# Set sizes 22, 14 and 8 in the last feed-forward, and weight differences formed later, in a two-layer encoder

## The chip, the cores and the metric

The kernel runs on one core of one Trainium2 chip. The metric is the device time of one execution in microseconds (us). Engines are named as in the profile: PE is TensorE (PEld its weight loads), DVE VectorE, ACT ScalarE, POOL GpSimd, SP SyncE, which here only issues transfers.

## The reference

272 tokens (16 learned ones and 256 given ones) of width 2048 go through two layers. Each has a mixing half (attention and a Fourier branch) and a feed-forward of inner width 5632:

```python
for i in range(DEPTH):
    h = _rmsnorm(h_stream, norm_mix[i])
    proj = h @ w_in[i]
    ...                                  # attention, Fourier branch, gates
    h_stream = h_stream + merged @ w_out[i]

    h2 = _rmsnorm(h_stream, norm_ffn[i])
    up = h2 @ w_up[i]
    u_gate = _dwconv3_centred(up[..., :D_FF], w_conv[i], b_conv[i])
    u_val = up[..., D_FF:]
    h_stream = h_stream + (jax.nn.silu(u_gate) * u_val) @ w_down[i]
return h_stream[:, N_META:]
```

All arrays are float32. In the last layer only the 256 given tokens are needed behind the feed-forward.

## The kernel before

Every weight arrives as chunks of 128 x 1024 float32 (512 KB), in one list `order`, on SP's queue, into four `raw` buffers. ACT casts a chunk to a rounded copy `wh` (line 230), DVE forms the remainder `wl = raw - wh` (line 233), and PE multiplies with both, so that three products of rounded numbers give nearly float32's accuracy. `wh` and `wl` have three buffers each: a cast waits until PE has left the chunk three places earlier. `group` (from line 280) walks the chunks of one group of 256 output columns; behind every second pair of products it calls `step`, which lets one waiting piece of side work be written down. A scheduler then sets the order on each engine from what depends on what; each engine works through its own list in that order.

The feed-forward has 44 inner tiles of 128, taken in sets: 24 and 20 in layer 0; 16, 16 and 12 in layer 1. For two inner tiles there is a group `ug` (gate half) and a group `uv` (value half) of four chunks each; here these eight are called U chunks. In layer 0 a set's down-projection `d` follows each set.

In layer 1 the first two sets are down-projected in another way. Two inner tiles by two halves of the tokens, times two inner tiles by two halves of the output, are 2 x 2 blocks, and seven block products do for eight. `PRODUCTS` lists the seven and the blocks to which each is added. Each needs a sum of activation blocks (`combos`, on DVE and ACT, up to four pairs of inner tiles at a time, tile `cb`) and a sum of weight blocks. A weight chunk of such a product is called an X chunk here: six matmuls of 128 x 512 (line 1046). The X chunks of a set are spread among the U chunks of the next set: 56 among 64 in the second set, 56 among 48 in the third. When a product is complete, `gather` adds its two 512-wide halves to `C4` (line 1030). The third set's down-projection `d` comes last as ordinary chunks (D chunks), eight groups of three; `turned` transposes `C4` into the result meanwhile.

Four of the seven weight operands are differences of blocks, and they don't depend on the tokens. `weight_sums` forms them during layer 0's feed-forward: for each pair of inner tiles it loads four blocks into `b0` to `b3` (on ACT's queue, line 977), subtracts four times on DVE (line 980) and writes the results to DRAM tiles `ts` (ACT's queue, line 982). It is a generator that `step` resumes; its `yield 9` and `yield 2` count such steps, four to a chunk. Layer 1 reads the `ts` tiles as X chunks.

Of the kernel before, what the change touches and what calls it, by code (L numbers as in the profile page):

```python
# [10 lines left out]
F32 = mybir.dt.float32  # L11
F32R = mybir.dt.float32r
AF = mybir.ActivationFunctionType
ALU = mybir.AluOpType
AX = mybir.AxisListType

P = 128
D = 2048
# [13 lines left out]
GRID_W = 64  # L32
CW = 4
MG = 2
FF_SPLIT = ((24, 20), (16, 16, 12))
NPR = sum(FF_SPLIT[-1][:2]) // 2
PRODUCTS = ((1, "11 12 21 22"), (2, "11"), (6, "12 21 22"), (7, "21 22"), (4, "21"), (5, "12 22"), (3, "12"))
PRE = 26
# [9 lines left out]
)  # L48
GN = max(FF_SPLIT[-1][2] * 2, FF_SPLIT[-1][0]) * SEQ + 64
G_LAST = 0  # L50
# [70 lines left out]
def encoder_kernel(ctx, tc, xT, params, consts, bmat, w_in, w_abr, w_four, w_f64, w_out, w_up, w_down, w_blk, outT):  # L121
    nc = tc.nc
    dram = ctx.enter_context(tc.tile_pool(name="dram", bufs=1, space=bass.MemoryType.DRAM))
    tsum = [[dram.tile([P, D // 2], F32, name=f"ts{q}_{e}") for e in range(4)] for q in range(NPR)]
# [7 lines left out]
    for l in range(DEPTH):  # L132
# [17 lines left out]
        k0 = 0  # L150
        for c, n in enumerate(FF_SPLIT[l]):
            ups = []
# [3 lines left out]
            if l == DEPTH - 1 and c:  # L156
                xs_, q0 = [], (k0 - FF_SPLIT[l][c - 1]) // 2
                for p, _ in PRODUCTS:
                    for q in range(FF_SPLIT[l][c - 1] // 2):
                        src = {1: w_blk[2 * (q0 + q), 0], 2: w_blk[2 * (q0 + q) + 1, 0], 3: w_blk[2 * (q0 + q) + 1, 1],  # L160
# [14 lines left out]
            order += ups  # L175
            if l < DEPTH - 1 or c == len(FF_SPLIT[l]) - 1:
                for mg in range(8):
# [5 lines left out]
    st = {"raw": 0, "fetch": 0, "next": 0, "grp": 0}  # L183
# [13 lines left out]
    def advance(upto):  # L197
        while st["raw"] < min(upto + RAW, len(chunks)):
            load_raw(st["raw"])
            st["raw"] += 1  # L200
        while st["fetch"] < min(upto, len(chunks)):
            i = st["fetch"]
            if i in folded:
                todo.append((i, lambda i=i: fold_w(i)))
            todo.append((i, lambda i=i: split_w(i, 0, CW)))
            st["fetch"] += 1
# [14 lines left out]
    def split_w(i, a, b, eng=None):  # L221
        if i not in splits:
            h = wp.tile([P, CW, MG * P], F32R, tag="wh", name=f"wh{i}")
            lo = wp.tile([P, CW * MG * P + 64], F32R, tag="wl", name=f"wl{i}")
            o = wl_at[i]
            splits[i] = h, lo[:, o:o + CW * MG * P].rearrange("p (c m) -> p c m", c=CW)
        h, lo = splits[i]
        r = raws[i]
        if eng is None:
            nc.scalar.copy(h[:, a:b], r[:, a:b])  # L230
        else:
            eng.tensor_copy(h[:, a:b], r[:, a:b])
        nc.vector.tensor_tensor(lo[:, a:b], r[:, a:b], h[:, a:b].bitcast(F32), op=ALU.subtract)  # L233
        if b == CW:
            del raws[i]
# [112 lines left out]
    def first_groups(pss):  # L348
# [17 lines left out]
        for i, c0, c1, ks in ((0, 0, 1, (0,)), (0, 1, 2, (1,)), (1, 0, 2, ()), (0, 2, 4, (2, 3)), (1, 2, 4, ())):  # L366
            for k in ks:
                norm_split(k, P_NM)
            split_w(i, c0, c1, nc.vector if (i, c0) == (0, 0) else None)
# [56 lines left out]
    small = ctx.enter_context(tc.tile_pool(name="small", bufs=4))  # L426
# [92 lines left out]
    for l in range(DEPTH):  # L519
# [7 lines left out]
        with tc.tile_pool(name=f"mix{l}", bufs=1) as mp:  # L527
# [394 lines left out]
            for half in range(2):  # L922
                mH = mL = None
                for kind, i in BRANCH_ORDER[half]:
# [19 lines left out]
                    else:  # L944
# [6 lines left out]
                        for m in range(MG):  # L951
                            k = 2 * j + m
                            t_, h_ = tha[i][:, m, lo:T], mH[:, k, lo:T]
# [13 lines left out]
        with tc.tile_pool(name=f"ffn{l}", bufs=1) as fp:  # L967
# [2 lines left out]

            def weight_sums():
                tt = nc.vector.tensor_tensor
                for q in range(NPR):
                    b = [fp.tile([P, D // 2], F32, tag=f"b{e}", name=f"b{e}") for e in range(4)]
                    for e, sums in ((0, ()), (1, ((0, 1, 0, 0),)), (3, ((1, 3, 1, 1), (3, 3, 0, 2))), (2, ((2, 2, 3, 3),))):
                        nc.scalar.copy(b[e][:, 0:1], st["cur"][:, 0, 0:1].bitcast(F32))
                        nc.scalar.dma_start(b[e], w_blk[2 * q + e // 2, e % 2])
                        yield 9
                        for o, x, y, to in sums:
                            tt(b[o], b[x], b[y], op=ALU.subtract)  # L980
                            yield 2
                            nc.scalar.dma_start(tsum[q][to], b[o])
                        yield 3

            sets, prods = [], {"have": {}}
            if last:
# [79 lines left out]
            if l == DEPTH - 2:  # L1066
                behindhand.append([24, weight_sums()])
# [142 lines left out]
```

## Time and profile before

| | us |
|---|---|
| median of 3 runs (2524.92 to 2531.62) | 2525.16 |
| the profiled execution, its own time | 2528.11 |
| its span, first to last instruction | 2526.0 |
| PE busy | 2511.2 |
| DVE busy | 1852.2 |
| ACT busy | 1276.4 |

The core's granted clock was 0.999 over the span. The span lies 2.1 us below the execution's own time, which lies 2.95 us above the median of the runs. Layer 0's feed-forward runs from about 522 to 1306 us. In layer 1's, the U chunks start at about 1804 us, the first X chunk at 1985.4 us and the D chunks at 2453.4 us. A row of the waits reads: who waited, for whom, us in total, times, longest. A row of the timeline reads: start, duration, engine, line, operation, tiles, and in brackets how long the engine was idle before it and what ended that.

### The profile page before, as it was taken

To read this page: it belongs to the slowest core of one execution; us is meant where nothing else is said; L and a number is where in the kernel's file an instruction comes from. 1 tells how busy PE (TensorE), PEld (TensorE's weight loads), DVE (VectorE), ACT (ScalarE), POOL (GpSimd) and SP (SyncE) were. 2 spreads that over 40 slices of the span, in tenths; PEclk is the share of its full clock that TensorE was granted. 3 is DMA by queue.
4 is the path that set the end of the run, shared out by engine and by line. 5 is a ranking of instruction groups with operands and counts; after the bars stand their busy time and mean duration, and the time that the engine had idled before them with its cause. 6 is when DMAs were issued, how large, how long until landed. Compare 5 with 4: busy or idle time off the path is not lost.

```text
span 2526.0 us, 47879 instructions
## 1 busy us (share of the span) xinstructions
PE 2511.2 (99%) x19404; PEld 2441.2 (97%) x19404; DVE 1852.2 (73%) x2851; ACT 1276.4 (51%) x1857; POOL 18.3 (1%) x37
## 2 busy tenths in 40 slices
PE   9999999999999999999999999999999999999999
PEld 9999999999999999999999999999999989988888
DVE  7687867776776556676556887677766788879985
ACT  6455544554444334444444564445644565556653
POOL 0000000000000000000000000000000000000000
PEclk9999999999999999999999999999999999999999
DMA  7545666568888887787554555666656677778875
GB/s 240 166 157 161 194 185 190 189 225 283 286 282 281 277 292 266 270 288 266 183 179 151 175 157 188 196 201 200 188 189 192 217 243 247 244 249 256 260 244 174
DMA packets 157501, 557.63 MB, mean 221 GB/s; under 512 B 18144, under 2 KB 22112, under 8 KB 157280
## 3 DMA queue, kind: packets, MB, share of 16 engines
q1 hardware_dynamic: 134480, 482.54, 59.5%
q10 hardware_dynamic: 22800, 72.04, 8.1%
q8 instruction: 152, 2.49, 0.4%
q14 instruction: 69, 0.57, 0.1%
HBM read 516.07 MB, written 35.65 MB: 218 GB/s over the span
## 4 chain that ended last, share of the span: by engine, by line
PE 95%; DVE 2%; DMA 1%; ACT 1%; issue 1%; ACTq 0%; SPq 0%; DVEq 0%
PE ps_ug L306 6%; PE ps_ug L304 6%; PE ps_uv L300 6%; PE ps_ug L305 6%; PE ps_x L1046 6%; PE ps_d L306 4%; PE ps_d L304 4%; PE ps_d L305 4%; PE ps_uv L301 3%; PE ps_uv L306 3%; PE ps_uv L304 3%; PE ps_uv L305 3%; PE ps_o L304 2%; PE ps_o L306 2%; PE ps_o L305 2%; PE ps_gf L304 2%
## 5 line engine op out<-in xcount | busy, mean ns | idle before, releaser
L233 DVE TENSOR_TENSOR wl<-raw,wh 128x1024 fp32r<-128x1024 f32 (+1 forms) x883 | 1073.8, 1220 | 442.5 <-ACT wh L230 438.2
L230 ACT CAST wh<-raw 128x1024 fp32r<-128x1024 f32 (+1 forms) x882 | 920.9, 1046 | 853.6 <-PE ps_ug L305 171.4
L306 PE MATMUL ps_ug<-xHL,wl 128*128 128x272 f32 (+1 forms) x1408 | 397.6, 282 | 2.7 <-DVE wl L233 2.7
L304 PE MATMUL ps_ug<-xHL,wh 128*128 128x272 f32 (+1 forms) x1408 | 399.1, 283 | 0.0
L305 PE MATMUL ps_ug<-xHL,wh 128*128 128x272 f32 (+1 forms) x1408 | 397.1, 282 | 0.0
L306 PEld LDWEIGHTS ps_ug<-xHL,wl 128*128 128x128 f32 x1408 | 264.5, 188 | 3.1 <-DVE wl L233 3.1
L305 PEld LDWEIGHTS ps_ug<-xHL,wh 128*128 128x128 f32 x1408 | 264.8, 188 | 2.2
L304 PEld LDWEIGHTS ps_ug<-xHL,wh 128*128 128x128 f32 x1408 | 264.3, 188 | 2.7
L300 PE MATMUL ps_uv<-xHL,wh 128*128 128x512 f32 x704 | 247.7, 392 | 0.0
L306 PE MATMUL ps_d<-gHL,wl 128*128 128x272 f32 (+1 forms) x728 | 208.3, 286 | 2.5 <-DVE wl L233 2.5
L304 PE MATMUL ps_d<-gHL,wh 128*128 128x272 f32 (+1 forms) x728 | 208.8, 287 | 0.0
L305 PE MATMUL ps_d<-gHL,wh 128*128 128x272 f32 (+1 forms) x728 | 207.4, 285 | 0.0
L304 PE MATMUL ps_uv<-xHL,wh 128*128 128x272 f32 x704 | 201.3, 286 | 0.0
L306 PE MATMUL ps_uv<-xHL,wl 128*128 128x272 f32 x704 | 200.7, 285 | 0.0
L305 PE MATMUL ps_uv<-xHL,wh 128*128 128x272 f32 x704 | 199.9, 284 | 0.0
L301 PE MATMUL ps_uv<-xHL,wl 128*128 128x256 f32 x704 | 198.3, 282 | 0.0
L300 PEld LDWEIGHTS ps_uv<-xHL,wh 128*128 128x128 f32 x704 | 132.0, 188 | 28.6
L1046 PE MATMUL ps_x<-wh,cb 128*128 128x512 f32 x448 | 156.6, 393 | 0.0
L304 PE MATMUL ps_ga<-xHL,wh 128*128 128x272 f32 (+1 forms) x512 | 147.0, 287 | 0.0
L304 PE MATMUL ps_gf<-xHL,wh 128*128 128x272 f32 (+1 forms) x512 | 145.8, 285 | 0.1
L304 PE MATMUL ps_o<-mH,wh 128*128 128x272 f32 (+1 forms) x512 | 144.6, 282 | 0.0
L306 PE MATMUL ps_ga<-xHL,wl 128*128 128x272 f32 (+1 forms) x512 | 144.6, 282 | 0.0
(306 smaller groups left out, 5979.8 us busy)
## 6 DMA issues: line engine op xcount, KB each, us to landing
raw<-in_w_up SPq DMA_DIRECT2D x352, 512.0 KB, 4.4
raw<-in_w_in SPq DMA_DIRECT2D x206, 512.0 KB, 3.6
raw<-in_w_down SPq DMA_DIRECT2D x112, 512.0 KB, 4.3
raw<-in_w_out SPq DMA_DIRECT2D x64, 512.0 KB, 3.9
b<-in_w_blk ACTq DMA_DIRECT2D x64, 512.0 KB, 5.0
ts<-b ACTq DMA_DIRECT2D x64, 512.0 KB, 3.6
raw<-ts SPq DMA_DIRECT2D x64, 512.0 KB, 4.5
raw<-in_w_blk SPq DMA_DIRECT2D x48, 512.0 KB, 4.4
```

The source lines that it names most:

```text
L230: nc.scalar.copy(h[:, a:b], r[:, a:b])
L233: nc.vector.tensor_tensor(lo[:, a:b], r[:, a:b], h[:, a:b].bitcast(F32), op=ALU.subtract)
L300: nc.tensor.matmul(o2, h[:, c, sl], ab, start=kt == 0, stop=False)
L301: nc.tensor.matmul(o, lo[:, c, sl], ab[:, 0, :], start=False, stop=kt == nk - 1)
L304: nc.tensor.matmul(o, h[:, c, sl], a, start=kt == 0, stop=False)
L305: nc.tensor.matmul(o, h[:, c, sl], b, start=False, stop=False)
L306: nc.tensor.matmul(o, lo[:, c, sl], a, start=False, stop=kt == nk - 1)
L1046: nc.tensor.matmul(ps[e], cb[:, s_, q - q4], w, start=q == 0 and a == 0, stop=q == n - 1 and a == 2)
```

## The change

The sets of layer 1 become 22, 14 and 8 inner tiles. There are 18 pairs in block products, not 16: 77 X chunks among 56 U chunks in the second set, 49 among 32 in the third, and 16 D chunks for 24. `weight_sums` treats two pairs more, and each of its subtractions is written down one load later than before: the sums that a load makes possible go into `due`, and they are formed behind the next load. The subtraction is now `x * one - y`, where `one` is a column of 128 ones, which ACT makes from the newest `wh` (0 times it plus 1). The numbers computed are the same.

```diff
-FF_SPLIT = ((24, 20), (16, 16, 12))
+FF_SPLIT = ((24, 20), (22, 14, 8))
...
             splits[i] = h, lo[...]
+            st["new"] = h
...
             def weight_sums():
                 tt = nc.vector.tensor_tensor
-                for q in range(NPR):
-                    b = [fp.tile([P, D // 2], F32, tag=f"b{e}", name=f"b{e}") for e in range(4)]
+                b, due = {}, []
+                for q in range(NPR + 1):
                     for e, sums in ((0, ()), (1, ((0, 1, 0, 0),)), (3, ((1, 3, 1, 1), (3, 3, 0, 2))), (2, ((2, 2, 3, 3),))):
-                        nc.scalar.copy(b[e][:, 0:1], st["cur"][:, 0, 0:1].bitcast(F32))
-                        nc.scalar.dma_start(b[e], w_blk[2 * q + e // 2, e % 2])
-                        yield 9
-                        for o, x, y, to in sums:
-                            tt(b[o], b[x], b[y], op=ALU.subtract)
-                            yield 2
-                            nc.scalar.dma_start(tsum[q][to], b[o])
-                        yield 3
+                        if q < NPR:
+                            t_ = fp.tile([P, D // 2], F32, tag=f"b{e}", name=f"b{e}")
+                            nc.scalar.copy(t_[:, 0:1], st["cur"][:, 0, 0:1].bitcast(F32))
+                            nc.scalar.dma_start(t_, w_blk[2 * q + e // 2, e % 2])
+                        yield 5
+                        if due:
+                            one = small.tile([P, 32], F32, tag="one", name="one", bufs=2)[:, 0:1]
+                            nc.scalar.activation(one, st["new"][:, 0, 0:1].bitcast(F32), AF.Identity, bias=1.0, scale=0.0)
+                        for o, x, y, to in due:
+                            nc.vector.scalar_tensor_tensor(o, x, one, y, op0=ALU.mult, op1=ALU.subtract)
+                            yield 3
+                            nc.scalar.dma_start(to, o)
+                        if q == NPR:
+                            return
+                        b[e] = t_
+                        yield 8 - 3 * min(len(due), 2)
+                        due = [(b[o], b[x], b[y], tsum[q][to]) for o, x, y, to in sums]
```

The two tiles of `one` take 256 bytes of a partition, and every tile of the mixing halves and feed-forwards moves up by 256 bytes; in layer 1's feed-forward the tiles behind the first set move by other whole multiples of 256.

How the order moves, first on ACT and DVE at the first subtraction in layer 0's feed-forward. Numbers behind `wh`, `wl` and `raw` count chunks; `b0` and `b1` are loaded blocks. ACT before:

```order
L230 CAST wh176_7020<-raw176_6859 128x1024
L976 COPY b1_7007<-wh176_7020 128x1
L977 DMA b1_7007<-in_w_blk 128x1024
L230 CAST wh177_7050<-raw177_6893 128x1024
L1129 CAST gHL_6785<-cv_6930 128x272
L230 CAST wh178_7088<-raw178_6946 128x1024
L982 DMA ts0_0_57<-b0_7006 128x1024
```

DVE before, at the same place:

```order
L233 TENSOR_TENSOR wl176_7021<-raw176_6859,wh176_7020 128x1024
L233 TENSOR_TENSOR wl177_7051<-raw177_6893,wh177_7050 128x1024
L1127 TENSOR_TENSOR cv_6930<-cv_6930,ps_0_uv_0_0_6944 128x272
L980 TENSOR_TENSOR b0_7006<-b1_7007,b0_7006 128x1024
L1130 TENSOR_TENSOR gHL_6785<-cv_6930,gHL_6785 128x272
L1127 TENSOR_TENSOR cv_6938<-cv_6938,ps_0_uv_0_1_6945 128x272
L233 TENSOR_TENSOR wl178_7089<-raw178_6946,wh178_7088 128x1024
```

ACT now, at the load of the same block:

```order
L231 CAST wh177_7055<-raw177_6901 128x1024
L979 COPY b1_7123<-wh177_7055 128x1
L980 DMA b1_7123<-in_w_blk 128x1024
L1139 CAST gHL_6793<-cv_6938 128x272
L231 CAST wh178_7093<-raw178_6954 128x1024
```

DVE now, at the first subtraction:

```order
L234 TENSOR_TENSOR wl182_7235<-raw182_7085,wh182_7234 128x1024
L1122 TENSOR_TENSOR cv_7210<-cv_7210,rstdB_149 128x272
L1119 SCALAR_TENSOR_TENSOR cv_7218<-u_7216,prm_142,cv_7218 128x271
L1120 SCALAR_TENSOR_TENSOR cv_7218<-u_7216,prm_142,cv_7218 128x271
L234 TENSOR_TENSOR wl183_7268<-raw183_7115,wh183_7267 128x1024
L1122 TENSOR_TENSOR cv_7218<-cv_7218,rstdB_149 128x272
L986 SCALAR_TENSOR_TENSOR b0_7014<-b1_7123,one_7283,b0_7014 128x1024
L234 TENSOR_TENSOR wl184_7301<-raw184_7148,wh184_7300 128x1024
```

Before, block b1 is asked for behind the cast of chunk 176 and used behind the remainder of chunk 177. Now it is asked for behind the cast of chunk 177 and used behind the remainder of chunk 183. Over the whole order, the number of remainders that DVE forms between a load's issue and the subtraction that needs it is 2 (53 times) or 3 (11 times) before, and 7 (64 times) or 8 (8 times) now.

Second, SP's queue in layer 1's third set, where the third of the seven products (`ts.._2`) is under way and then the fourth (`ts.._1`) begins. Chunks from `in_w_up` are U chunks, from `ts` X chunks. Before:

```order
L190 DMA raw814_27319<-ts8_2_91 128x1024
L190 DMA raw815_27349<-in_w_up 128x1024
L190 DMA raw816_27379<-ts9_2_95 128x1024
L190 DMA raw817_27401<-in_w_up 128x1024
L190 DMA raw818_27413<-ts10_2_99 128x1024
L190 DMA raw819_27425<-in_w_up 128x1024
L190 DMA raw820_27453<-ts11_2_103 128x1024
L190 DMA raw821_27467<-in_w_up 128x1024
L190 DMA raw822_27489<-ts12_2_107 128x1024
L190 DMA raw823_27501<-in_w_up 128x1024
L190 DMA raw824_27523<-ts13_2_111 128x1024
L190 DMA raw825_27549<-ts14_2_115 128x1024
```

Now:

```order
L190 DMA raw845_28075<-ts11_2_103 128x1024
L190 DMA raw846_28103<-ts12_2_107 128x1024
L190 DMA raw847_28115<-in_w_up 128x1024
L190 DMA raw848_28141<-ts13_2_111 128x1024
L190 DMA raw849_28171<-in_w_up 128x1024
L190 DMA raw850_28183<-ts14_2_115 128x1024
L190 DMA raw851_28219<-ts15_2_119 128x1024
L190 DMA raw852_28233<-in_w_up 128x1024
L190 DMA raw853_28245<-ts16_2_123 128x1024
L190 DMA raw854_28275<-in_w_up 128x1024
L190 DMA raw855_28287<-ts17_2_127 128x1024
L190 DMA raw856_28317<-ts11_1_102 128x1024
```

Two X chunks in a row stand eight times in the old third set (56 X on 48 U chunks) and never in the old second set; now they stand 21 times in the second set (77 on 56) and 17 times in the third (49 on 32). Three in a row stand nowhere in either.

## The prediction

> **What bounds the kernel now.** First the page: span, busy time, granted clock, chain of waits.
>
> ```profile
> span 2526.0 us, 47879 instructions
> PE 2511.2 (99%) x19404; PEld 2441.2 (97%) x19404; DVE 1852.2 (73%) x2851; ACT 1276.4 (51%) x1857; POOL 18.3 (1%) x37
> PEclk9999999999999999999999999999999999999999
> PE 95%; DVE 2%; DMA 1%; ACT 1%; issue 1%; ACTq 0%; SPq 0%; DVEq 0%
> ```
>
> TensorE sets the end: 95% of the chain is its own work, at full clock. A change helps if it takes matmul time away or closes one of the few places where TensorE stands still. So next come windows: the later part of layer 0's feed-forward, then layer 1's second and third sets.
>
> ```profile
> 804.00:1190.00 386.00, 380.86 (x3101) 380.05 (x3100) 252.09 (x306) 165.11 (x226) 0.00 (x0) 1.00 0.81 276
> 1983.00:2243.00 260.00, 260.00 (x1638) 234.64 (x1636) 211.31 (x267) 156.49 (x194) 0.00 (x0) 1.00 0.79 243
> 2243.00:2453.40 210.40, 210.40 (x1278) 187.60 (x1277) 182.27 (x236) 130.04 (x161) 0.00 (x0) 1.00 0.81 257
> ```
>
> A row gives the length, the busy time of PE, PEld, DVE, ACT and POOL, the clock, the transfer engines' share and GB/s. In layer 1's two sets TensorE never stands still, though VectorE is busy for 81% and 87% of them. In layer 0 it loses 386.00 - 380.86 = 5.1 us. The view of waits says for what: PE's own for 520 to 1310 us, then DVE's and ACT's largest on transfers.
>
> ```profile
> PE ps_ug L306 <- DVE wl L233: 2.7, 2, 1.7
> PE ps_d L306 <- DVE wl L233: 2.5, 1, 2.5
> ```
>
> ```profile
> DVE b L980 <- DMA b<-in_w_blk: 69.3, 44, 4.9
> ACT wh L230 <- DMA raw<-in_w_up: 3.3, 5, 1.1
> ```
>
> Three waits for a remainder `wl`, 5.2 us together. The timeline of the longest, from ACT, DVE and PE:
>
> ```profile
> 1176.38 0.34 ACTq L977 DMA_DIRECT2D b<-in_w_blk  x1
> 1184.35 1.23 DVE L980 TENSOR_TENSOR b<-b,b 128x1024 f32<-128x1024 f32 x1 [4.86 <-DMA b<-in_w_blk]
> 1185.49 1.22 DVE L233 TENSOR_TENSOR wl<-raw,wh 128x1024 fp32r<-128x1024 f32 x1
> 1186.04 1.04 ACT L230 CAST wh<-raw 128x1024 fp32r<-128x1024 f32 x1 [6.63 <-DVE b L980]
> 1186.77 0.39 PE L306 MATMUL ps_d<-gHL,wl 128*128 128x272 f32 x1 [2.46 <-DVE wl L233]
> ```
>
> A block asked for at 1176.38 lets the subtraction start at 1184.35, 8.0 us later. The subtraction is at the head of DVE's list; the remainder that TensorE needs stands behind it, and so, behind the write-out of the difference, does ACT's next cast.
>
> **The change, part by part.** *Later differences.* Between a load and its subtraction now stand 7 or 8 remainders, not 2 or 3. In the first window TensorE takes 380.86 / 3101 = 0.123 us for a matmul, 24 of them to a chunk, 2.95 us: the subtraction now comes some 20 us behind the load. The landings of the `b` tiles' transfers:
>
> ```profile
> DMA to landing us min/median/max: 2.6/4.6/7.9
> ```
>
> 20 us is well over 7.9, so DVE's 69.3 us of waiting should go, and TensorE's three waits with it: -5.2 us. The bounds are -5.2 and 0, the latter if the wait only changes hands. Added are eight subtractions, and all 72 have a new form, whose price at this size the trace doesn't show. The nearest rows compare the two forms at 256 elements, and give the old one at 1024:
>
> ```profile
> L1109 DVE SCALAR_TENSOR_TENSOR cv<-u,prm,cv 128x256 f32<-128x256 f32 x44 | 21.1, 481 | 0.7 <-ACT cv L1107 0.2
> L1112 DVE TENSOR_TENSOR cv<-cv,rstdB 128x256 f32<-128x256 f32 x44 | 18.5, 419 | 0.2 <-ACT cv L1111 0.2
> L980 DVE TENSOR_TENSOR b<-b,b 128x1024 f32<-128x1024 f32 x64 | 78.4, 1224 | 69.7 <-DMA b<-in_w_blk 69.3
> ```
>
> From 62 ns more each (a fixed part) to 15% more (by size), 1.29 to 1.41 us; 72 of those less 64 x 1.22 put 14 to 23 us on DVE over some 690 us, where the window shows it idle for 35%. I cost that at nothing; it is the cover that the vanished waits leave. The 54 columns of `one` are copies of one element per partition on ACT, idle for 57% there. The wait they add, of DVE for ACT, ends early: `one` stands behind a cast whose remainder, 1.22 us of DVE's time, is ahead of the subtraction. Behind the subtraction wait further remainders, as before. The 16 transfers more (8 loads, 8 writes on ACT's queue) raise the rate there by 16/392, from 276 to at most 287 GB/s.
>
> *Two more pairs as block products.* 14 X chunks come, 8 D chunks go, and fewer U chunks are followed by an X chunk (88 for 104). Chunk times are read as steps between first matmuls, on PE's timeline:
>
> ```profile
> 1815.98 0.39 PE L300 MATMUL ps_uv<-xHL,wh 128*128 128x512 f32 x1
> 1818.76 0.39 PE L300 MATMUL ps_uv<-xHL,wh 128*128 128x512 f32 x1
> 2432.49 0.28 PE L304 MATMUL ps_ug<-xHL,wh 128*128 128x258 f32 x1
> 2435.32 0.39 PE L1046 MATMUL ps_x<-wh,cb 128*128 128x512 f32 x1
> 2449.22 0.40 PE L300 MATMUL ps_uv<-xHL,wh 128*128 128x512 f32 x1
> 2452.01 0.40 PE L1046 MATMUL ps_x<-wh,cb 128*128 128x512 f32 x1
> 2453.39 0.39 PE L300 MATMUL ps_d<-gHL,wh 128*128 128x512 f32 x1
> 2464.24 0.39 PE L300 MATMUL ps_d<-gHL,wh 128*128 128x512 f32 x1
> 2466.96 0.39 PE L300 MATMUL ps_d<-gHL,wh 128*128 128x512 f32 x1
> ```
>
> A U chunk takes 2.78 us among its own kind (1815.98 to 1818.76), ahead of an X chunk 2.83 (`ug`) or 2.79 (`uv`); an X chunk 1.38; a D chunk 2.72. So 14 x 1.38 - 8 x 2.72 = -2.4 us, and 16 transitions less (12 behind `ug` at 0.05, 4 behind `uv` at 0.01) another -0.6: -3.0 us. The same by the Trainium skill, "TensorE: Matmul & The Clock Gate", Back-to-back issue gap, whose isolated gap is N/2.4 + 2.5 ns: 216 ns at 512 columns and 109 at 256 would give -2.7 for the first part, an estimate; the page also gives 131 ns for 512 in a stream with weight loads, against 1.38/6 = 0.23 us here, so the trace decides.
>
> *Feeding the denser sets.* This is the cost. Pairs of X chunks in a row go from 8 to 38. Behind a pair, the next U chunk's cast must wait until TensorE leaves the U chunk ahead of the pair (three buffers); then two X chunks, 2.77 us, have to cover a cast and a remainder:
>
> ```profile
> L230 ACT CAST wh<-raw 128x1024 fp32r<-128x1024 f32 x878 | 918.7, 1048 | 852.7 <-PE ps_ug L305 171.4 <-PE ps_d L305 125.1 <-PE ps_uv L300 81.5
> L233 DVE TENSOR_TENSOR wl<-raw,wh 128x1024 fp32r<-128x1024 f32 x878 | 1070.9, 1224 | 441.7 <-ACT wh L230 437.4
> ```
>
> 1.05 + 1.22 us and the hand-overs leave some 0.3 us. Of the eight pairs of before, one shows a loss, on PE's timeline:
>
> ```profile
> 2299.31 0.40 PE L300 MATMUL ps_uv<-xHL,wh 128*128 128x512 f32 x1
> 2299.93 0.39 PE L300 MATMUL ps_uv<-xHL,wh 128*128 128x512 f32 x1
> ```
>
> 0.62 us for two matmuls that otherwise take 2.78/8 = 0.35: 0.27 us. VectorE's steps in a row (1024, 512, 256 elements):
>
> ```profile
> 2388.26 2.35 DVE L233 TENSOR_TENSOR wl<-raw,wh 128x1024 fp32r<-128x1024 f32 x2
> 2425.37 1.28 DVE L1030 TENSOR_TENSOR C<-C,ps_x 128x512 f32<-128x512 f32 x2
> 2465.14 0.74 DVE L1147 TENSOR_TENSOR XT<-XT,ps_d 128x256 f32<-128x256 f32 x2
> ```
>
> Less one busy time each that is 1.13, 0.60 and 0.33 us. The third set loses 23 chunks of 1.13 and two `ug`/`uv` pairs' evaluation (ten steps of 0.33, four of some 0.4: 4.9 us): DVE 182.3 - 26.0 - 9.8 - 1.8 (smaller sums) = 144.7 us, PE 210.4 - 16 x 2.78 - 7 x 1.38 = 156.3 us: 93%, from 87%. The second set: (211.3 + 13 x 1.13 + 6.6 - 4.2) / (260.0 + 21 x 1.38 - 8 x 2.78) = 228.4 / 266.7, 86%. Worst is the second of seven products in the third set, where eight halves of the first (8 x 0.60) meet the sums for the third (3 x 1.07): DVE 13.1 + 2.8 + 8.0 = 23.9 us in 22.4 us of PE. Before, the same place needed 29.4 in 30.2, and the one loss fell there. Bounds: 0, if the scheduler places this work as luckily as at seven pairs of eight; 38 x 0.27 = 10.3 if every pair costs what that one did. I take near the lower end, 38 x 0.27/8 = 1.3, and 0.6 for the overloaded product: +1.9 us.
>
> *The end.* The first D group has two chunks, not three, to cover the last evaluation and the transposes; the work is the same. I take 0, and at most the 2.7 us of the missing chunk.
>
> Sum: -5.2 - 3.0 + 1.9 = -6.3 us. The profiled execution (2528.1, span 2526.0) would become 2521.8 with a span of 2519.7; on the median of 2525.16, the time is **2518.9 us**.
>
> **The rivals.**
> A: as summed, 2518.9 (2516.5 to 2521.5). 0.50.
> B: no loss in feeding: 2525.2 - 8.2 = 2517.0. For it: seven pairs of eight lost nothing. Against: 93% and 107%. 0.17.
> C: the differences bring half or less. The profiled execution lies 2.95 us above the median, so the timed ones may lose less than 5.2 to waits, or the wait goes to ACT, whose write-outs still stand right behind the subtractions. -2.3 - 3.0 + 1.9 = -3.4 at 2521.8; none at all, 2524.1. Against: the two low runs are alike within 0.3 us, as with waits that recur. 0.20.
> D: feeding binds. Each of the 38 pairs costs TensorE 0.27 us, at the U chunk behind the pair: -8.2 + 10.3 = +2.1, 2527.3, slower than before. It decides from 8.2/38 = 0.22 us per pair on. For it: 0.3 us to spare, and ACT already waited five times (3.3 us) for weights that had not landed, at 257 GB/s; the sets now ask for 133 x 0.524 MB / 266.7 us = 261 and 81 x 0.524 / 156.3 = 272 GB/s. Against: 276 GB/s in layer 0 with landings of 4.6 us. The Trainium skill, "DMA: Bandwidth & Descriptors", Latency and other measured facts, speaks for D: a transfer's fixed part grows with the load on HBM (0.2 us on average, 2 at high load); the spread from 2.6 to 7.9 us agrees with that, without showing the cause. 0.13.
>
> **How the numbers follow.** A change of 0.3%, 7.6 us, is about what a measurement of this kernel can tell from none: faster means under 2517.6, slower over 2532.7. A's lower part (0.20) and most of B (0.14) are faster, with a little of unforeseen gain: 0.36. D with more lost than at that one pair, or a shift by 256 bytes that makes reads slower everywhere (no row shows such a thing), gives 0.06 slower. The rest, 0.58, is no change. The range is 2514.5 to 2526.5: it leaves out D's upper half and gains beyond B.
>
> **What would show it.** Right: no wait of DVE `b` on a transfer; no PE wait for `wl` in layer 0's feed-forward, so that PE busy in 804 to 1190 us is nearly the window; 126 X chunks at 1.38 us; steps of 0.6 us behind X pairs in a few places, most in the third set's second product. Wrong: PE waits for `wl` there that add up to more than 5 us; ACT waiting for `one`'s users or for `b`'s write-outs; casts that wait for `raw` by tens of us; another step between matmuls in stages that the change doesn't touch.

## The result and the profile after

| | us |
|---|---|
| kernel before, median of 6 runs (2524.9 to 2532.36) | 2525.55 |
| changed kernel, median of 6 runs (2514.5 to 2518.34) | 2517.95 |
| ratio of the two, with its 95% interval | 0.9962 (0.9949 to 0.9975) |
| the profiled execution of the changed kernel, its own time and its span | 2518.24, 2516.3 |

The prediction was 2518.9 (2514.5 to 2526.5). First the page of the changed kernel, then windows (columns as before): the same stretch of layer 0's feed-forward as was shown of before, then layer 1's second and third sets from their first U chunk on.

```profile
span 2516.3 us, 48010 instructions
PE 2505.9 (100%) x19352; PEld 2434.4 (97%) x19352; DVE 1872.6 (74%) x2875; ACT 1292.8 (51%) x1928; POOL 18.3 (1%) x37
```

```profile
804.00:1190.00 386.00, 386.00 (x3161) 386.00 (x3160) 263.34 (x314) 174.64 (x265) 0.00 (x0) 1.00 0.86 290
2042.79:2307.41 264.62, 264.41 (x1584) 234.86 (x1583) 220.46 (x276) 168.02 (x205) 0.00 (x0) 1.00 0.80 262
2307.41:2465.43 158.02, 157.99 (x935) 139.57 (x934) 144.34 (x189) 101.24 (x124) 0.00 (x0) 1.00 0.83 268
```

In 804 to 1190 us TensorE no longer stands still: it does 3161 matmuls where it did 3101. VectorE has 83% and 91% of the two sets to do, where the prediction had 86% and 93%. DVE's waits in 516 to 1310 us, the three longest and the one that is left of the subtraction's, and the groups of the `b` tiles:

```profile
DVE wl L234 <- ACT wh L231: 199.4, 184, 1.7
DVE u L1115 <- PE ps_ug L307: 12.8, 17, 2.2
DVE XT L1163 <- PE ps_d L307: 7.0, 13, 2.2
...
DVE b L986 <- ACT one L984: 3.2, 3, 1.3
```

```profile
L986 DVE SCALAR_TENSOR_TENSOR b<-b,one,b x72: 1277/1279/1286, 566.1 to 1231.8; 128x1024 f32<-128x1024 f32 x72
...
DMA to landing us min/median/max: 2.9/5.2/8.9
```

The 69.3 us that the subtraction waited for transfers are gone, and 3.2 us for `one` stand there instead. The new form takes 1.28 us, a little under the 1.29 of the prediction's lower bound. Of PE there is no wait left in this stretch. So where did the time go? The first matmuls of layer 0's feed-forward (`ug`), of layer 1's mixing half (`f`), of layer 1's feed-forward and of its D chunks, on PE's timeline; before:

```profile
522.51 0.29 PE L304 MATMUL ps_ug<-xHL,wh 128*128 128x272 f32 x1
1305.56 0.29 PE L304 MATMUL ps_f<-xHL,wh 128*128 128x272 f32 x1
1804.05 0.28 PE L304 MATMUL ps_ug<-xHL,wh 128*128 128x258 f32 x1
```

(the D chunks of before start at 2453.39, in a row of the prediction), and after:

```profile
524.50 0.29 PE L305 MATMUL ps_ug<-xHL,wh 128*128 128x272 f32 x1
1299.73 0.29 PE L305 MATMUL ps_f<-xHL,wh 128*128 128x272 f32 x1
1797.44 0.28 PE L305 MATMUL ps_ug<-xHL,wh 128*128 128x258 f32 x1
2465.45 0.39 PE L301 MATMUL ps_d<-gHL,wh 128*128 128x512 f32 x1
```

| stage, us | before | after | difference |
|---|---|---|---|
| up to layer 0's feed-forward | 522.5 | 524.5 | +2.0 |
| layer 0's feed-forward | 783.0 | 775.2 | -7.8 |
| layer 1's mixing half | 498.5 | 497.7 | -0.8 |
| layer 1's U and X chunks | 649.4 | 668.0 | +18.7 |
| D chunks, to PE's last matmul | 69.5 | 47.6 | -21.9 |
| rest of the span | 3.2 | 3.3 | +0.1 |

Layer 0 gave 7.8 us (forecast 5.2), layer 1's feed-forward 3.2 (forecast 1.1). The mixing halves do the same work and differ by waits of under 1 us at a few places, as they also do between the experiments' runs (522.0 to 524.0 us up to layer 0's feed-forward where the byte places are those of the change or of before; 524.5 here).

### The profile page after: what moved, and what is told of

It is laid out like the page before. It is cut to its first block, busy times and chain, and to the rows that moved or that the text cites. A ratio compares the mean times of both kernels' runs of the same rounds, so it can differ in the third digit from the quotient of the medians.

```text
span 2516.3 us, 48010 instructions
## 1 busy us (share of the span) xinstructions
PE 2505.9 (100%) x19352; PEld 2434.4 (97%) x19352; DVE 1872.6 (74%) x2875; ACT 1292.8 (51%) x1928; POOL 18.3 (1%) x37
## 4 chain that ended last, share of the span: by engine, by line
PE 94%; DVE 3%; DMA 1%; ACT 1%; issue 1%; ACTq 0%; SPq 0%; DVEq 0%
PE ps_ug L307 7%; PE ps_x L1056 7%; PE ps_ug L305 7%; PE ps_ug L306 7%; PE ps_uv L301 6%; PE ps_d L307 4%; PE ps_d L305 4%; PE ps_d L306 3%; PE ps_uv L305 3%; PE ps_uv L307 3%; PE ps_uv L306 3%; PE ps_uv L302 3%; PE ps_o L305 2%; PE ps_o L307 2%; PE ps_o L306 2%; PE ps_gf L305 2%
## 5 line engine op out<-in xcount | busy, mean ns | idle before, releaser
L305 PE MATMUL ps_d<-gHL,wh 128*128 128x272 f32 (+1 forms) x720 | 205.8, 286 | 0.0
L306 PE MATMUL ps_d<-gHL,wh 128*128 128x272 f32 (+1 forms) x720 | 204.4, 284 | 0.0
L1056 PE MATMUL ps_x<-wh,cb 128*128 128x512 f32 x504 | 171.0, 392 | 0.0
```

Source lines behind the costliest of these rows:

```text
L305: nc.tensor.matmul(o, h[:, c, sl], a, start=kt == 0, stop=False)
L306: nc.tensor.matmul(o, h[:, c, sl], b, start=False, stop=False)
L1056: nc.tensor.matmul(ps[e], cb[:, s_, q - q4], w, start=q == 0 and a == 0, stop=q == n - 1 and a == 2)
```

## The experiments

Each expectation names its theories as they stood before the run. A ratio is to the kernel before, run on the same chip.

**The two halves of the change apart.** First the later differences with the old sets:

```diff
-FF_SPLIT = ((24, 20), (22, 14, 8))
+FF_SPLIT = ((24, 20), (16, 16, 12))
```

> The later differences alone: the sets stay 16, 16 and 12, 64 subtractions, each 7 or 8 remainders behind its load. Theory (the late subtraction takes away the waits for transfers): layer 0's feed-forward gets 5 to 8 us shorter (the trace of the change shows 7.8 there, the prediction's term was 5.2), DVE does not wait for a transfer of b at all, PE not for wl in 520 to 1310 us, and layer 1's feed-forward stays at 718.8 us within 0.5; time 2517.5 to 2520.3, a ratio to the kernel before of 0.997 to 0.998. Rival (the 7.8 us of layer 0 came from what the new sets change there too, such as places in memory): layer 0's feed-forward is shorter by less than 2 us and a wait for wl stays; time 2523 to 2525.

Measured: 2519.92 us, ratio 0.9974 (0.9965 to 0.9983). Layer 0's feed-forward takes 775.2 us, as in the change, and layer 1's 719.1. PE waits for nothing in 520 to 1310 us. Then the new sets with the old differences (the kernel before, with the one line turned the other way):

> The sets 22, 14 and 8 alone, with the differences formed as before (72 of them, 1 to 3 remainders behind the load). Theory: layer 1's feed-forward gets 3.2 us shorter, as in the trace of the change (the prediction's terms: -3.0 + 1.9 = -1.1); layer 0's keeps its waits and, with eight subtractions more, gains up to an eighth of them, +0.7: time 2522 to 2525, ratio 0.9985 to 1.000, DVE waiting some 70 to 80 us for transfers of b. Rival (the sets bring the whole gain of the change): time 2518, no wait of PE for wl in layer 0.

Measured: 2525.93 us, ratio 1.0001 (0.9986 to 1.0016). PE's waits in 516 to 1310 us, and DVE's for the blocks:

```profile
PE ps_d L306 <- DVE wl L233: 3.0, 2, 2.6
PE ps_uv L306 <- DVE wl L233: 2.2, 2, 1.5
PE ps_ug L306 <- DVE wl L233: 1.8, 1, 1.8
```

```profile
DVE b L980 <- DMA b<-in_w_blk: 81.1, 50, 4.3
```

Layer 0's feed-forward takes 784.8 us, 1.8 more than before, since two more pairs bring more of the same waits; layer 1's takes 715.8, 3.0 less. So the late subtraction alone explains layer 0, and the sets' gain in layer 1 is real, but with early subtractions most of it is spent in layer 0, and the time shows no gain. The first theory held in the first run. In the second its mechanism held, but the time lies just outside its 2522 to 2525: layer 0 lost 1.8 us, not up to 0.7.

**What holds the subtraction back.** The operand `one` replaced by a plain subtraction:

```diff
-nc.vector.scalar_tensor_tensor(o, x, one, y, op0=ALU.mult, op1=ALU.subtract)
+tt(o, x, y, op=ALU.subtract)
```

> The changed kernel with a plain subtraction x - y in place of x * one - y; the column of ones is still made but nothing reads it. It is written down as late as in the change, but the scheduler puts it 2 remainders behind the load (61 of 72 times; 3 eight times, 1 three times), not 7 or 8. Theory (what counts is the place in DVE's list, and it is the column of ones that holds the subtraction back): DVE's waits for b return, 60 to 80 us, and PE's for wl, 3 to 8 us; time as with the sets alone, 2521 to 2525. Rival (the written place or the form of the instruction counts): no such wait, time 2517 to 2519.

Measured: 2534.8 us, ratio 1.0037 (1.0023 to 1.0052): the first theory's waits, but TensorE's add up to 12.7 us where it had 3 to 8, and the time is 10 us over its range. Layer 0's feed-forward takes 792.3 us. PE's waits there, and DVE's for the blocks:

```profile
PE ps_uv L307 <- DVE wl L234: 9.4, 7, 4.1
PE ps_d L307 <- DVE wl L234: 2.5, 2, 1.7
PE ps_ug L307 <- DVE wl L234: 0.8, 1, 0.8
```

```profile
DVE b L986 <- DMA b<-in_w_blk: 69.1, 42, 4.1
```

The longest of them, from ACT's and DVE's timelines:

```profile
1107.57 0.34 ACTq L980 DMA_DIRECT2D b<-in_w_blk  x1
...
1115.46 0.33 ACTq L988 DMA_DIRECT2D ts<-b  x1
1115.89 1.05 ACT L231 CAST wh<-raw 128x1024 fp32r<-128x1024 f32 x1 [3.94 <-DVE b L986]
```

```profile
1114.21 1.23 DVE L986 TENSOR_TENSOR b<-b,b 128x1024 f32<-128x1024 f32 x1 [3.50 <-DMA b<-in_w_blk]
1115.35 1.22 DVE L234 TENSOR_TENSOR wl<-raw,wh 128x1024 fp32r<-128x1024 f32 x1
```

The block is asked for at 1107.57 and used 6.6 us later; the remainder waits on DVE behind the subtraction, and the next cast on ACT behind the write-out. Without an operand that is made late, the subtraction ends up mostly 2 remainders behind its load, whether the program writes it where the kernel before does or one load later. Why this version loses more than the sets with the old differences (17.0 us against the change's layer 0, 9.6 there) is open in part: the waits are of the same kind, at other places of the lists, and the longest is followed by 13 matmuls at about half the clock (0.51 granted in 1117 to 1120 us), 1.4 us that no row of waits counts.

**How late is late enough.** The sums of a block formed behind its own load again, with `one`, 9 steps behind it in the first run and 3 in the second:

```diff
-                        yield 5
+                        yield 9      # 3 in the second run
+                        ...          # b[e] = t_, and due = the sums of this block
                         if due:
                             one = ...
                         for o, x, y, to in due:
                             ...
-                            yield 3
+                            yield 2
                             nc.scalar.dma_start(to, o)
-                        ...
-                        yield 8 - 3 * min(len(due), 2)
-                        due = ...
+                        yield 3
```

> The changed kernel with the sums formed behind their own load again, 9 steps behind it as before, but in the new form with the column of ones: all 72 subtractions stand 5 remainders behind the load, 5 x 2.95 = 14.8 us. Theory (the subtraction has only to come later than the slowest landing, 8.9 us in the trace of the change): no wait of DVE for b, no wait of PE for wl, time as in the change, 2516.5 to 2519.5. Rival (all 7 or 8 are needed, since the write-out, the next load and the subtraction share the tiles): waits return, over 10 us on DVE, time 2520 or more.

> The kernel of the run with the sums behind their own load, but formed 3 steps behind it, not 9: the subtractions stand 3 remainders behind the load (51 of 72 times; 4 or 5 twenty times, 2 once), about 3 x 2.95 = 8.9 us, less what ACT runs ahead. Theory (the place counts against the landing, median 5.2 and at most 8.0 to 8.9 us): only a few waits of DVE for b, under 10 us together, and at most one wait of PE for wl; time 2517 to 2520. Rival (the two blocks and the write-out need the 5 places): DVE waits for b by 40 us or more, time 2521 to 2526.

Measured: 2517.31 us, ratio 0.9964 (0.9952 to 0.9976), and 2517.03 us, ratio 0.9966 (0.9953 to 0.9978). Layer 0's feed-forward takes 775.24 us in both; with 3 remainders DVE's waits and the landings are:

```profile
DVE b L990 <- DMA b<-in_w_blk: 4.4, 9, 1.0
```

```profile
DMA to landing us min/median/max: 3.4/6.6/8.7
```

Nine short waits, and none reaches TensorE. At 2 remainders (the kernel before, the sets alone, the plain subtraction) DVE waits 69 to 81 us, at 3 it waits 4.4, at 5 and at 7 not at all. The 7 or 8 of the change are more than it needs; what counts is that three chunks, 8.8 us, just about cover the slowest landing. The first theory held in both runs.

**How dense the sets may get.** Two runs with 20 pairs and 8 D chunks, then two with the change's 18 pairs and 16 D chunks, spread in other ways:

```diff
-FF_SPLIT = ((24, 20), (22, 14, 8))
+FF_SPLIT = ((24, 20), (20, 20, 4))      # then (24, 16, 4), (16, 20, 8), (20, 16, 8)
```

With 20 pairs `yield 8 - ...` is 7 as well, so that all the sums fit into layer 0.

> The changed kernel with sets of 20, 20 and 4 inner tiles: 20 pairs in block products, 70 X chunks among 80 U chunks in the second set (no two in a row), 70 among 16 in the third (runs of four and five), 8 D chunks. 80 subtractions, 6 to 8 remainders behind their loads. Theory (a chunk behind two X chunks fits the 2.77 us of the pair as long as DVE has room; DVE by the sum of the changed kernel's third set, 135.3 - 9.8 + 5.7 + 6.3 = 137.5 us of some 141, 97%): 14 X chunks at 1.38 more, 8 D chunks (21.9 us) less, -2.5 us against the change, and up to 3 lost where the evaluation, the sums and the first D group of one chunk meet: 2514 to 2519. Rival D (each chunk behind two X chunks costs 0.27 us; there are some 70 of them): +16 us, 2531 or more, with waits of PE for wl all over the third set.

> The same with sets of 24, 16 and 4: 84 X chunks among 64 U chunks in the second set (20 pairs in a row), 56 among 16 in the third (runs of three and four), 8 D chunks; DVE in the third set 135.3 - 9.8 - 10.2 + 2.1 = 117.4 us of some 122, 96%. Theory: as with 20, 20 and 4, 2514 to 2519, the second set without a loss over 1 us. Rival D: some 60 chunks behind two X chunks at 0.27, +14 us, 2529 or more.

> The changed kernel with sets of 16, 20 and 8: 18 pairs and 16 D chunks as in the change, but 56 X chunks among 80 U chunks in the second set and 70 among 32 in the third, 2.2 to one (the change has 1.5, 24, 16 and 4 had 3.5), in runs of two and three. DVE there by the sum of the change's third set: 144.3 + 23.7 + 6.3 = 174 us of 185.5, 94%, against 91% in the change and 103% with 24, 16 and 4. Theory (the loss comes where DVE has more to do than TensorE): third set at most 5 us over its chunks' own time, time 2518 to 2523. Rival (runs of three X chunks are what cannot be fed): some 20 runs of three at 0.5 us and more, 10 us or more lost, 2528 or more.

> The changed kernel with sets of 20, 16 and 8: the same 126 X chunks and 16 D chunks, 70 among 64 U chunks in the second set and 56 among 32 in the third, 1.75 to one; 6 pairs of X chunks in a row in the second set and 24 in the third, none of three. DVE in the third set 144.3 + 7.9 + 2.1 = 154 us of 166, 93%. Theory (DVE's load decides): third set 1.5 to 4 us over its chunks' own time, as in the change or a little more; one time of 2516 to 2521. Rival (each pair costs 0.27 us): 30 pairs for 38, 2 us less than the change.

Measured (the times are of different chips, on which the kernel before had medians of 2525.3 to 2528.8 us, so the ratios and the excess are what can be compared; the excess is a set's length less 2.774 us for each U chunk and 1.382 for each X chunk; DVE is its busy time as a share of those chunks' own time, in the third set):

| sets | time, us | ratio | X per U, 2nd set: excess | X per U, 3rd set: excess | DVE |
|---|---|---|---|---|---|
| 16, 16, 12 (before) | 2525.55 | 1 | 0.88: 2.9 | 1.17: 2.3 | 88% |
| 22, 14, 8 (the change) | 2517.95 | 0.9962 | 1.38: 2.9 | 1.53: 1.5 | 92% |
| 20, 16, 8 | 2518.07 (one run) | - | 1.09: 3.0 | 1.75: 2.4 | 93% |
| 16, 20, 8 | 2522.64 | 0.9976 (0.9965 to 0.9987) | 0.70: 2.9 | 2.19: 7.8 | 93% |
| 24, 16, 4 | 2533.26 | 1.0034 (1.0021 to 1.0047) | 1.31: 3.2 | 3.50: 19.6 | 103% |
| 20, 20, 4 | 2542.68 | 1.0069 (1.0055 to 1.0083) | 0.88: 3.6 | 4.38: 29.4 | 104% |

Windows of the third sets of 24, 16, 4 and of 16, 20, 8:

```profile
2358.83:2500.22 141.39, 130.46 (x657) 105.38 (x656) 125.84 (x153) 88.12 (x101) 0.00 (x0) 0.98 0.80 265
```

```profile
2276.06:2469.36 193.30, 190.40 (x1063) 162.74 (x1061) 172.72 (x220) 125.19 (x153) 0.00 (x0) 1.00 0.84 275
```

PE's waits in the third set of 20, 20, 4:

```profile
PE ps_x L1056 <- DVE wl L234: 4.8, 12, 0.8
PE ps_uv L301 <- ACT wh L231: 4.7, 3, 2.0
PE ps_x L1056 <- DVE C L1040: 4.3, 1, 4.3
PE ps_uv L302 <- DVE wl L234: 1.6, 3, 0.9
PE ps_x L1056 <- ACT wh L231: 0.3, 1, 0.3
```

With 20 pairs the theory failed and the times are in rival D's range, with more lost than its 16 and 14 us: the 2.5 us of work saved are lost eight to twelve times over, nearly all of it in the third set. TensorE waits for remainders, for casts and for a product's halves to leave PSUM (`C`, line 1040). These rows add up to 15.7 us of the 29.4; behind three of the waits (2.0, 4.3 and 1.9 us) follow spells at a lower granted clock, about 1.5 us each, and 0.97 is granted over the set. In both third sets DVE has more to do than TensorE, 103% and 104%, where the sums ahead of the runs had 96% and 97%. But the mean load alone does not decide: at 93% the sets 20, 16, 8 lose next to nothing and 16, 20, 8 lose 7.8 us, which lies between what the two theories gave. What differs is how X chunks stand: behind the 32 U chunks of the former come 24 pairs and eight single ones, of the latter 26 pairs and six runs of three (the "some 20" of the expectation was a miscount). In the latter no U chunk is left with less than two X chunks behind it, and the remainder of a U chunk ends on the median 0.2 us after TensorE has started on the chunk; with 20, 16, 8 it ends 0.25 us ahead of that, in the change 0.4 us. That this lack of places to catch up, and not a product of ten X chunks with ten pairs' sums to form, makes the difference is argued only. Pairs with room between them cost nothing that shows: the second set of 24, 16, 4 has 20 pairs and an excess of 3.2 us, against 2.9 of before with none.

**The byte places.** The change moves the tiles behind `one` by 256 bytes. With columns of 64, 192 and 32 bytes they move by 128, 384 and 64:

```diff
-one = small.tile([P, 32], F32, tag="one", name="one", bufs=2)[:, 0:1]
+one = small.tile([P, 16], F32, tag="one", name="one", bufs=2)[:, 0:1]      # then 48, 8
```

> The changed kernel with columns of ones of 64 bytes in place of 128, so that every tile behind them moves up by 128 bytes in a partition, not by 256. Nothing else differs. Theory (the place in a partition by 128 bytes more or less has no price): time as the change, 2516 to 2520. Rival (what TensorE reads must stand at certain places, and 256 keeps them while 128 doesn't): matmul steps get longer in stages that the change does not touch, the mixing halves among them; more than 2524.

> The changed kernel with columns of ones of 192 bytes, so that every tile behind them moves up by 384 bytes. Theory (the matmuls of the down-projections are slower when their tile of activations stands at an odd multiple of 128 bytes from where it stood; places count by their remainder in 256): as with 128 bytes, time 2526 to 2532, a chunk of the down-projection at 2.80 us in layer 1, layer 0's feed-forward at 782. Rival (128 bytes made another tile collide, and larger distances are free): as the change, 2516 to 2520, 2.72 us.

> The changed kernel with columns of ones of 32 bytes, so that every tile behind them moves up by 64 bytes. Theory (remainder in 256 counts, and only the kernel's own places are the good ones): slower than the change in the same matmuls, by about as much as 128 bytes or less, 2520 to 2530. Rival (64 bytes are below what TensorE's reads notice): as the change, 2516 to 2520.

Measured: 2528.68 us, ratio 1.0011 (1.0000 to 1.0022); 2528.78 us, ratio 1.0001 (0.9989 to 1.0012); 2529.59 us, ratio 1.0000 (0.9986 to 1.0015). Their spans are 10 to 12 us longer than the change's (2526.4, 2528.3 and 2526.4 for 2516.3), with the same instructions. Windows in layer 0's feed-forward, 200 us of U chunks and 100 us of D chunks; the change, then 128, 384 and 64 bytes:

```profile
560.00:760.00 200.00, 200.00 (x1638) 200.00 (x1637) 148.26 (x194) 98.27 (x158) 0.00 (x0) 1.00 0.85 288
1195.00:1295.00 100.00, 100.00 (x821) 100.00 (x820) 62.41 (x80) 47.32 (x69) 0.00 (x0) 1.00 0.68 223
```

```profile
560.00:760.00 200.00, 200.00 (x1639) 200.00 (x1638) 148.25 (x194) 98.25 (x158) 0.00 (x0) 1.00 0.84 288
1195.00:1295.00 100.00, 100.00 (x798) 100.00 (x798) 61.86 (x79) 45.89 (x68) 0.00 (x0) 1.00 0.69 229
```

```profile
1195.00:1295.00 100.00, 100.00 (x799) 100.00 (x798) 62.32 (x80) 46.57 (x69) 0.00 (x0) 1.00 0.69 226
```

```profile
1195.00:1295.00 100.00, 100.00 (x805) 100.00 (x805) 62.56 (x81) 47.36 (x69) 0.00 (x0) 1.00 0.68 227
```

TensorE is busy throughout at full clock in all of them; it does fewer D matmuls in the same time, 798 for 821, and as many U matmuls. From first matmul to first matmul a D chunk takes 2.933 us in the change, 3.013 with 128 and with 384 bytes, 2.987 with 64; an `o` chunk of layer 0's mixing half 2.933, then 2.987 in all three; a U chunk 2.933 always. 88 D chunks at 0.080 are 7.0 us, just what layer 0's feed-forward is longer (782.3 for 775.2). 128 and 384 bytes do the same, 256 bytes nothing: the place counts by its remainder in 256 as far as these four show. The theory for 128 bytes failed and its rival held; the theory for 384 bytes held, with D chunks of layer 1 at 2.80 us for 2.72; that for 64 bytes held in its time and in layer 0. So that the two columns take 256 bytes, and not 64, 128 or 384, is worth some 10 us, more than the change's gain.

## Why the prediction was right, and where it was not

- **The differences, -5.2: right mechanism, too small.** It measured -7.8 in the stage, and the run with the later differences alone shows the same 7.8. The term was mis-sized because the loss was read off the busy time (386.00 less 380.86) and the three recorded waits (5.2), as if TensorE ran at full pace beside them. The count of matmuls in the same window gives more: 60 more in 386 us, at 386.00 / 3161 = 0.122 us, are 7.3 us. Of the stage's 7.8 us, 5.2 are the recorded waits, 1.6 come from a slow spell behind the longest of them, and about 1 from slips under 0.3 us each. PE's timeline of before, 0.9 us behind the end of that wait, and a window in the spell:

```profile
1187.64 0.43 PE L306 MATMUL ps_d<-gHL,wl 128*128 128x272 f32 x1
...
1191.03 0.29 PE L306 MATMUL ps_d<-gHL,wl 128*128 128x272 f32 x1
```

```profile
1189.00:1191.00 2.00, 2.00 (x10) 2.00 (x10) 1.36 (x4) 1.64 (x4) 0.00 (x0) 0.50 0.99 317
```

  The 15 matmuls from 1187.64 to 1191.03 take 3.39 us, 0.226 each, where 15 x 0.122 would be 1.83: 1.6 us more, at a granted clock of 0.50, with TensorE shown as busy all the time. The prediction's "at full clock" missed this; a mean over 386 us still reads 1.00. The timed runs lose about as much as the profiled one: 0.26% of 2525 is 6.6 us (0.17% to 0.35%, 4.3 to 8.8). With that rival C falls.
- **The order of events was right**: no wait of DVE for a transfer, none of PE for `wl`, the subtraction over 8.9 us behind its load, `one` without a price (3.2 us of DVE waits, none passed on). The new form at 1.28 us costs DVE 72 x 1.28 - 64 x 1.22 = 14 us, all under cover. The rate rose to 290 GB/s in the window, not "at most 287".
- **Fourteen X chunks for eight D chunks, -2.4**: 14 x 1.382 - 21.87 = -2.5.
- **Transitions -0.6 and feeding +1.9, together +1.3: wrong.** The second and third sets' excess went from 2.88 + 2.32 to 2.86 + 1.53 us, -0.8. The fewer transitions are in that; the feeding cost under 1 us. The prediction's gap of some 0.3 us was right: behind 27 of the 38 pairs the remainder was ready 0.14 to 0.37 us ahead of TensorE, behind seven it came later, and only three places lost over 0.15 us (0.37, 0.17 and 0.20). What failed is the 0.6 us for the overloaded product, which is not there, and the price of 0.27 us per eighth pair. The largest of the three was not DVE's doing. ACT's timeline and then PE's at this place:

```profile
2131.89 1.05 ACT L231 CAST wh<-raw 128x1024 fp32r<-128x1024 f32 x1 [2.60 <-DMA raw<-in_w_up]
2133.13 1.05 ACT L231 CAST wh<-raw 128x1024 fp32r<-128x1024 f32 x1 [0.19 <-DMA raw<-ts]
```

```profile
2133.77 0.28 PE L306 MATMUL ps_ug<-xHL,wh 128*128 128x258 f32 x1
2134.25 0.39 PE L307 MATMUL ps_ug<-xHL,wl 128*128 128x258 f32 x1 [0.20 <-DVE wl L234]
```

  A chunk had landed late, the cast with it, and the first remainder of the `ug` chunk behind the pair came 0.37 us late.
- **The end, 0**: 47.59 us for 16 D chunks against 69.46 for 24 are 21.87 less, 8 x 2.73. Right.
- **Rivals.** The time lies in A's range, with B's reason (no loss in feeding). D is wrong for these sets, yet its mechanism exists: it decides from the third set of 16, 20, 8 on.
- **The sum.** Span 2519.7 was forecast for the profiled execution and 2516.3 measured, 3.4 less: -2.6 by the differences, -2.1 by the sets, +2.0 and -0.8 in mixing halves that the change does not touch, +0.1 at the end. That the median came within 1 us of the forecast is in part luck: the profiled execution came out 3.6 us below its own forecast (2518.24 for 2521.8), but before it lay 2.95 us above the median, and after it lies 0.29 above.

## What to carry to other kernels

Where a side transfer's user stands in the same in-order list as work that the bound engine waits for, count how much time lies between issue and use, against the slowest landing, not the median; a little more is enough (8.8 us here, for landings of up to 8.7), and a scheduler may undo the place that the program gives it, unless the instruction depends on something late. Read what a busy engine loses from its count of equal instructions in a fixed window, beside its busy time, and look at the granted clock in the few us behind each wait, not over the whole stage. When a small tile is added, keep every tile behind it at its old remainder in 256 bytes (four shifts show no more than that), or measure the matmuls that read them.

## What had not been expected of the hardware

**Places.** That some matmuls at full clock get 2 to 4% slower by a shift of 64 or 128 bytes (most for an `o` chunk of layer 1 with 64 bytes, 2.880 us for 2.773) was in no step of the prediction (it gave a shift by 256 bytes a small chance of harm, and that has none). Why is open: the runs moved all tiles of the pools together, and don't tell whether the place itself or the distance to the weights counts.

**The clock after a wait.** In the third set of 20, 20, 4 the 4.3 us wait for `C` was followed by slow matmuls; PE's timeline, and the window of 4 us behind it:

```profile
2441.13 0.77 PE L1056 MATMUL ps_x<-wh,cb 128*128 128x512 f32 x1 [4.29 <-DVE C L1040]
2441.69 0.63 PE L1056 MATMUL ps_x<-wl,cb 128*128 128x512 f32 x1
...
2444.15 0.39 PE L1056 MATMUL ps_x<-wl,cb 128*128 128x512 f32 x1
2444.37 0.61 PE L1056 MATMUL ps_x<-wh,cb 128*128 128x512 f32 x2
```

```profile
2441.00:2445.00 4.00, 3.87 (x11) 3.17 (x12) 2.37 (x4) 0.94 (x1) 0.00 (x0) 0.62 0.48 154
```

Until 2444.15 an X matmul takes about 0.43 us, then 0.23, and the granted clock over the window is 0.62. The Trainium skill, "TensorE: Matmul & The Clock Gate", What's actually happening, states half the rate after an idle window of about 3.4 us; this trace agrees, with 4.3 us of waiting. The spell costs about 1.4 us more than the wait shows. But the length of one wait does not decide here. The 2.46 us of the kernel before are less than the page's window and were followed by half the clock too (the lines under the differences above), and the measurement decides; 2.61 us in the run with the new sets alone were not, with 1.00 granted in 1241 to 1243 us:

```profile
1239.82 0.39 PE L306 MATMUL ps_d<-gHL,wl 128*128 128x272 f32 x1 [2.61 <-DVE wl L233]
```

What tells the two apart is open.
